# A decoder layer on one core: gated results transposed by DMA instead of TensorE, and low parts by accumulating DMAs in more blocks

## The chip, the core and the metric

The kernel runs on one core of a Trainium2 chip, in one launch. A core has engines with instruction streams of their own: TensorE (PE in the profile; PEld is its loading of the stationary operand), VectorE (DVE), ScalarE (ACT), GpSimd (POOL) and SyncE (SP). Each engine executes its instructions in order and waits on semaphores for the others. Transfers run on 16 DMA engines; they are issued from the streams of SP, ACT and POOL, also in order. The on-chip memory SBUF has 128 partitions; TensorE writes to PSUM, eight banks of 128x512 words of 32 bits.

The metric is the device time of a run in microseconds. The profile is one more execution, recorded instruction by instruction.

## What is computed

One layer of a decoder for 256 tokens of 2048 features, all in float32: a first gated feed-forward, two token mixers in parallel, a second gated feed-forward, and a gated embedding. The change touches the two feed-forwards:

```python
def swiglu(x, w_gu, w_down):
    g, u = jnp.split(x @ w_gu, 2, axis=-1)
    return (jax.nn.silu(g) * u) @ w_down
...
h = layer_norm(alpha * h + 0.5 * swiglu(h, w_ffn1_gu[i], w_ffn1_down[i]), ln_g[i, 0], ln_b[i, 0])
...
h = layer_norm(alpha * h + 0.5 * swiglu(h, w_ffn2_gu[i], w_ffn2_down[i]), ln_g[i, 2], ln_b[i, 2])
```

`x` is 256x2048, `w_gu` 2048x11264 (gate and up, 5632 columns each) and `w_down` 5632x2048. The middle of the layer (input projections, retention, attention, mixing) has the same form before and after the change.

## The kernel before, in words

**Numbers.** Every float32 operand is split into a high part in the matmul's own 32-bit format and a low part, the rest (`split`, L97 to L99: a copy on ScalarE at L98, a subtraction on VectorE at L99). A product is then three matmuls: low by high, high by high, high by low (`Sum.add`, L393 to L395).

**Weights.** They come in chunks of 128x1024 words, 512 KB, by DMAs from SP (L112). Four classes prepare them. `Single` (kind P) splits a chunk as above. `Folded` copies it to the high part on ScalarE (L162), writes the negated high part to the low tile on ScalarE (L163), and issues on POOL's queue a DMA that adds the raw chunk to it (L164): the subtraction runs in the DMA engines instead of VectorE. Kind F is a pair of one `Single` and one `Folded`, the gate's chunk and the up's chunk. `Seven` (kind S) takes the gate's and the up's chunk together and makes their four products of half blocks with seven products instead of eight: VectorE forms four sums (L189 to L192), and the parts are split on ScalarE and VectorE. `Prepared` (kind D) is the same with the sums made earlier in the run and loaded from HBM: six loads instead of two, and three splits.

**The gate and up stage.** A feed-forward handles its 5632 columns in eleven blocks, j = 0 to 10, of 512. A block has eight units, written as a string of eight letters by `gu_units` (L873 to L881): a unit P or F is two chunks of 12 matmuls each, a unit S or D one step of 21 matmuls. In the first feed-forward (names f1) blocks 1 to 10 are FFSSFSSF. In the second (f2) the blocks in `AHEAD` (1, 2, 3, 4, 5 and 7) are PPSDSDSP where j is odd and PPSSDSSP where j is even; block 6, 8 and 10 are PPSSPSSP and block 9 is PPSPSPSP. Block 0 has eight plain units in both.

**The end of a block.** The sums of the sevens are combined (`seven_common`), VectorE adds the rest from PSUM (L993), ScalarE applies Silu (L994) and VectorE multiplies gate and up (L995) into `v`: 256 tokens as two tiles of 128 partitions by 512 columns. The next stage needs it with the columns on the partitions. `turned` (L929 to L939) does that: eight transposes of 128x128 on TensorE into two PSUM banks (L937), and two copies on ScalarE into the tile `raw` of SBUF (L939). `convert` splits `raw` later, in the second stage (`w_down`), which starts with block 0's tile.

**The order.** No scheduler reorders: every stream has its instructions in the order in which the program's text issues them. After each chunk or step, `done` gives its SBUF slots back and calls `fill`, which issues the making of further chunks while the work made ahead is under 45 units (a chunk counts 12, a step 21), and loads while it is under 90. Then `run_side` takes one job from the list `side`. A job is put there by `later(n, job)`, as number n in the list (L1130 to L1134): the transposes of a block's result are issued with the third call of `run_side` in the next block, after its third chunk.

SBUF is shared out in 46 slots of 4 KB per partition (`SLOTS`); a new tile takes the slot that has been free longest, and its first writer waits for that slot's last reader.

Of the kernel before, what the change touches and what calls it, by code (L numbers as in the profile page):

```python
# [8 lines left out]
F32 = mybir.dt.float32  # L9
F32R = mybir.dt.float32r  # L10
I32 = mybir.dt.int32
AF = mybir.ActivationFunctionType
ALU = mybir.AluOpType
PSUM = bass.MemoryType.PSUM

P = 128
S = 256
# [23 lines left out]
SEVEN = (0, 1, 2, 3)  # L41

AHEAD = {1: (4, 5), 2: (4,), 3: (4, 5), 4: (4,), 5: (4, 5), 7: (4, 5)}
# [12 lines left out]
def layer(ctx: ExitStack, tc: tile.TileContext, io):  # L56
    nc = tc.nc
    sync, act, dve, pool, pe = nc.sync, nc.scalar, nc.vector, nc.gpsimd, nc.tensor
# [8 lines left out]
    def bank(name):  # L67
        return psum.tile([P, 512], F32, tag="ps", name=name)

    def banks(name):  # L70
        return [bank(name + str(j)) for j in range(2)]

    def slot(shape, dt, name):
        return slots.tile(shape, dt, tag="slot", name=name)

    def half(name):
        return slot([P, 2, 256], F32, name)
# [241 lines left out]
    def slots_for_weights(n, ahead=45, far=90):  # L319
        room.update(slots=n, ahead=ahead, far=far)  # L320
# [164 lines left out]
    def units_of(order, sevens, ahead=()):  # L485

        sevens, ahead = list(sevens), list(ahead)
        plain = [p for p in range(KD // 2) if p not in sevens + ahead]
        of = {"S": sevens, "D": ahead, "P": plain, "F": plain}
        return [(kind, of[kind].pop(0)) for kind in order]  # L490
# [61 lines left out]
    def rsqrt(dst, var, n, eps):  # L552
# [7 lines left out]
        )  # L560
        s = small.tile([P, n], I32, tag=f"ns{n}", name="ns", bufs=2)
        dve.tensor_scalar(s, v[:, 0].bitcast(I32), 1, None, ALU.logical_shift_right)
        y = small.tile([P, n], I32, tag=f"ny{n}", name="ny", bufs=2)
        dve.tensor_scalar(y, s, -1.0, float(0x5F3759DF - 2**31), ALU.mult, ALU.add)
# [37 lines left out]
    def ln_stats_by_root(stats, i, t, eps, between):  # L602
# [4 lines left out]
        root = small.tile([P, 1], F32, tag="nq1", name="nroot")  # L607
        act.activation(root, mv[:, 1:2], AF.Sqrt, bias=roots[eps], scale=4.0)
        v = small.tile([P, 1], F32, tag="nb1", name="nv")
# [10 lines left out]
    def table_of(f):  # L620

        act.activation(warm, warm, f)
# [29 lines left out]
    class Norm:  # L652
# [36 lines left out]
        def turn(self, t, c):  # L689

            args = self.y, t, self.i, self.new
            if c < 3 and (t, c + 1) != self.put_off:
                self.more(t, c + 1)
            self.sums_behind()
            if c == 0:
                for k0 in (0, 2):
                    ln_turn(*args, k0, 2, self.keep.get(c))
            else:
                ln_turn(*args, 4 * c, 4, self.keep.get(c))
# [19 lines left out]
        def run(self, steps, lhs, events, blks=(), calm=2):  # L719


            self.vectors = vectors.pop()
            table_of(AF.Sqrt)
            self.new = big.tile([P, KD, 512], F32R, tag="ht", name=f"ht{self.i}")
# [20 lines left out]
        def first(self, steps, lhs, sums, events):  # L745
# [14 lines left out]
            self.put_away()  # L760
            table_of(AF.Silu if self.i < 2 else AF.Sigmoid)

# [48 lines left out]
    ident = const.tile([P, P], F32, name="ident")  # L811
# [23 lines left out]
    def rotary_table(nm):  # L835

        inv, sgn = (0, 2) if nm == "r" else (1, 3)
        pos_i = slot([P, S], I32, "pos_i" + nm)
        act.dma_start(pos_i, io["positions"].broadcast_to([P, S]))
# [20 lines left out]
        yield  # L860
        act.activation(nb, n, AF.Sin)
        yield
# [5 lines left out]
        yield  # L868
        act.activation(cos, na, AF.Sin)
        yield  # L870


    def gu_units(name, j):  # L873
        if j == 0:
            return [("P", p) for p in range(KD // 2)]
        if name == "f2" and j in AHEAD:
            return units_of(*(("PPSDSDSP", SEVEN[:3]) if j % 2 else ("PPSSDSSP", SEVEN)), AHEAD[j])
        order = "PPSSPSSP" if j % 2 == 0 else "PPSPSPSP"
        if name == "f1":
            order = "FFSSFSSF"  # L880
        return units_of(order, SEVEN[: order.count("S")])  # L881

    def gu_keys(name, j):
        return lambda n, p: (name + "_gu", j, n, p)
# [34 lines left out]
    def ffn(name, i, ht, norm, keep, residual, keepers, away):  # L919
# [3 lines left out]
        raws = []  # L923
# [4 lines left out]

        def turned(j, v):  # L929

            raw = slot([P, 4, S], F32, f"{name}a{j}")
            raws.append(raw)
            ps = banks(f"{name}t{j}")
            for k in range(4):
                for t in range(2):
                    at = slice(k % 2 * S + t * P, k % 2 * S + t * P + P)
                    pe.transpose(ps[k // 2][:, at], v[:, t, k * P : (k + 1) * P], ident)  # L937
            for h in range(2):
                act.copy(raw[:, 2 * h : 2 * h + 2], ps[h].rearrange("p (b n) -> p b n", b=2))  # L939

        acts = {}

# [5 lines left out]
        for j in range(KF // 4):  # L948
            pg, pu = banks(f"{name}g{j}"), banks(f"{name}u{j}")
            units = gu_units(name, j)  # L950
            n_of = {(0, 0): KD, (0, 1): KD, (1, 0): KD, (1, 1): KD}
            for kind, p in units:
                if kind in "SD":
                    for at in ((0, 0), (0, 1), (1, 0)):
                        n_of[at] -= 1
                    n_of[1, 1] -= 2
            sums = [[Sum((pg, pu)[n][t], n_of[t, n]) for n in range(2)] for t in range(2)]
            got = []

            if norm is not None and j == 0:  # L960
                front, units = units[:FRONT_PAIRS], units[FRONT_PAIRS:]
                steps = [(gu_keys(name, 0)(n, p), 2 * p, n) for _, p in front for n in range(2)]
                norm.first(steps, rhs, sums, (
                    (3, (1, 0)), (5, "more"), (5, (1, 1)), (7, (0, 2)), (8, (1, 2)), (9, (0, 3)), (10, (1, 3)), (10, "go"),
                ))
                slots_for_weights(24)

            def before(u, j=j, offset=KD // 2 - len(units)):
                u += offset
                if j == 0 and norm is None and u % 2 == 0:  # L970
                    first_chunk(u // 2)
                    if u == 6:
                        slots_for_weights(24)
                    if u == 2:
                        load_constants()
                if j == 0 and u == 7:
                    for g in sorted({p // 2 for p in SEVEN}):
                        hi, lo = (slot([P, 8, P], F32R, f"{name}f{w}{g}") for w in "hl")
                        made[g] = seven_forms(keep[g], hi, lo)
                    if name == "f2":  # L980
                        g = AHEAD[1][0] // 2
                        made[g] = forms_of([ht[:, 4 * g : 4 * g + 4, :]], f"{name}f{g}")
                if name == "f2" and j in AHEAD and u == 0:
                    slots_for_weights(AHEAD_SLOTS - j)
                if j == KF // 4 - 1 and u in (4, 6):
                    convert(u // 2 - 2)

            block(f"{name}{j}", units, gu_keys(name, j), rhs, forms, sums, lambda *a: got.extend(seven_common(*a)), before)
            if got:
                g, v = got  # L990
                for x, ps in ((g, pg), (v, pu)):
                    for t in range(2):
                        dve.tensor_tensor(x[:, t], x[:, t], ps[t], ALU.add)  # L993
                act.activation(g, g, AF.Silu)  # L994
                dve.tensor_tensor(v, g, v, ALU.mult)  # L995
            else:
                v = slot([P, 2, 512], F32, f"{name}v{j}")
                for t in range(2):
                    act.activation(v[:, t], pg[t], AF.Silu)
                for t in range(2):  # L1000
                    dve.tensor_tensor(v[:, t], v[:, t], pu[t], ALU.mult)
            later(2, lambda j=j, v=v: turned(j, v))
        stats = small.tile([P, 2, 4, 6], F32, tag="stats", name=name + "st", bufs=1)

        def others(n, ahead=45):
# [77 lines left out]
    def joined(ps, name, dst=None):  # L1083
        lo = half(name + "lo")
        v = half(name + "v") if dst is None else dst
        for f in range(2):
            act.copy(lo[:, f], ps[f][:, S:])
            dve.tensor_tensor(v[:, f], ps[f][:, :S], lo[:, f], ALU.add)
        return v
# [40 lines left out]
    def later(n, job):  # L1130
        for j in range(n):
            if len(side) <= j:
                side.append(idle)
        side.insert(n, job)  # L1134
# [519 lines left out]
    def first_chunk(c):  # L1654

        if c == 0:
            load_x_chunk(0)
            fill()
        if c < 3:
            load_x_chunk(c + 1)  # L1660
# [157 lines left out]
```

## Time and profile before

| | |
|---|---|
| median of three runs | 2269.6 us (2269.53 to 2271.87) |
| the profiled execution | 2269.44 us |
| its span, first to last instruction | 2267.3 us |
| TensorE clock granted in it | 0.999 |
| moved by DMA | 536.69 MB, mean 237 GB/s |
| f1's gate and up stage, j = 1 to 10 | about 50 to 468 us of the span |
| f2's gate and up stage, j = 0 to 10 | about 1473 to 1933 us of the span |

How to read it. The span lies within the execution's own time; 2.1 us lie around it. A row of a group reads: line, engine, operation, output and inputs by the program's names, shapes, count | busy us, mean ns of one | idle time of that engine just before them, and what ended it. A row of a timeline reads: start in us, duration in us, engine, line, operation, names, count, and in brackets the idle time before it with its releaser. A row of a window reads: the stretch, its length, then busy us (and number of instructions) of PE, PEld, DVE, ACT and POOL, the granted clock, the share of time in which the 16 DMA engines were busy, and what they moved in GB/s. Matmuls are pipelined, so that durations of neighbours overlap; their distance is read from their starts.

### The profile page before, as it was taken

The numbers are of one execution on the slowest core, as the hardware profiler recorded it, in microseconds if no ns is written. First come the engines' busy times: TensorE is split into PE (matmuls) and PEld (weight loads), VectorE is DVE, ScalarE is ACT, GpSimd is POOL, SyncE is SP. The second block draws the span as 40 slices with busy tenths as digits, with TensorE's granted clock in tenths as the row PEclk, the third lists the DMA queues.
The fourth block names the chain that finished last, engine by engine and source line by source line (L and its number), as shares of the span: only waits on it lengthen the run. The fifth ranks groups of instructions, "written<-read, shape, count | busy, mean of one in ns | idle before, by whom it ended". The sixth has DMA issues, their size and how long they took to land.

```text
span 2267.3 us, 29270 instructions
## 1 busy us (share of the span) xinstructions
PE 2258.9 (100%) x10482; PEld 1877.7 (83%) x10482; DVE 1975.9 (87%) x2576; ACT 1272.5 (56%) x1543; POOL 37.1 (2%) x49
## 2 busy tenths in 40 slices
PE   9999999999999999999999999999999999999998
PEld 7888888888888888888778888888888888888887
DVE  7988989999989887888789788689999999889887
ACT  6676776656555444535566454455555565555543
POOL 0000010000000000000000000000000000000000
PEclk9999999999999999999999999999999999999999
DMA  9888898865677878775456568787867766555772
GB/s 316 249 261 252 238 262 243 250 208 186 216 285 261 291 282 289 256 236 183 140 158 225 183 211 293 271 288 247 297 242 250 255 197 218 196 190 209 290 269 73
DMA packets 216889, 536.69 MB, mean 237 GB/s; under 512 B 17052, under 2 KB 21532, under 8 KB 216744
## 3 DMA queue, kind: packets, MB, share of 16 engines
q1 hardware_dynamic: 209000, 511.28, 65.9%
q0 software_dynamic: 5760, 20.97, 5.1%
q10 hardware_dynamic: 1984, 2.58, 0.4%
q8 instruction: 82, 1.34, 0.2%
q14 instruction: 63, 0.52, 0.1%
HBM read 484.43 MB, written 29.36 MB: 227 GB/s over the span
## 4 chain that ended last, share of the span: by engine, by line
PE 78%; DVE 1%; DMA 1%; ACT 0%; issue 0%; ACTq 0%; DVEq 0%
PE f2g L395 3%; PE f2g L393 3%; PE f2g L394 3%; PE rqk L344 3%; PE f2u L393 2%; PE f2u L395 2%; PE f2u L394 2%; PE aqk L344 2%; PE f1d L395 2%; PE f2d L394 2%; PE f2d L395 2%; PE f1d L393 2%; PE f1d L394 2%; PE f2d L393 2%; PE f1e L395 1%; PE f2e L394 1%
## 5 line engine op out<-in xcount | busy, mean ns | idle before, releaser
L99 DVE TENSOR_TENSOR lf_gu<-rf_gu,hf_gu 128x1024 fp32r<-128x1024 f32 (+1 forms) x229 | 271.9, 1210 | 11.1 <-ACT hf_gu L98 10.4
L98 ACT CAST hf_gu<-rf_gu 128x1024 fp32r<-128x1024 f32 (+1 forms) x229 | 232.8, 1041 | 30.2 <-DMA rf_gu<-in_f_gu 29.9
L99 DVE TENSOR_TENSOR lf_down<-rf_down,hf_down 128x1024 fp32r<-128x1024 f32 x150 | 178.8, 1220 | 19.0 <-ACT hf_down L98 18.5
L99 DVE TENSOR_TENSOR lw_in_f<-rw_in_f,hw_in_f 128x1024 fp32r<-128x1024 f32 x140 | 167.5, 1220 | 25.0 <-ACT hw_in_f L98 24.7
L98 ACT CAST hf_down<-rf_down 128x1024 fp32r<-128x1024 f32 x150 | 151.7, 1049 | 50.7 <-DMA rf_down<-in_f_down 18.0
L98 ACT CAST huf_gu<-uf_gu 128x1024 fp32r<-128x1024 f32 x75 | 79.0, 1053 | 147.5 <-DVE uf_gu L190 138.0
L98 ACT CAST hw_in_f<-rw_in_f 128x1024 fp32r<-128x1024 f32 x140 | 140.3, 1050 | 3.2 <-PE rv L394 1.4
L98 ACT CAST hvf_gu<-vf_gu 128x1024 fp32r<-128x1024 f32 x75 | 79.1, 1055 | 31.7 <-DVE vf_gu L192 30.8
L99 DVE TENSOR_TENSOR luf_gu<-uf_gu,huf_gu 128x1024 fp32r<-128x1024 f32 x75 | 91.4, 1219 | 0.0
L99 DVE TENSOR_TENSOR lvf_gu<-vf_gu,hvf_gu 128x1024 fp32r<-128x1024 f32 x75 | 91.4, 1218 | 0.0
L393 PE MATMUL f1g<-hf_gu,xt 128*128 128x512 f32 x232 | 90.6, 390 | 0.2 <-ACT hf_gu L98 0.2
L395 PE MATMUL f1g<-lf_gu,xt 128*128 128x512 f32 x232 | 90.7, 391 | 0.0
L394 PE MATMUL f1g<-hf_gu,xt 128*128 128x512 f32 x232 | 90.4, 390 | 0.0
L393 PE MATMUL f2g<-hf_gu,ht 128*128 128x512 f32 x217 | 84.7, 390 | 0.0
L395 PE MATMUL f2g<-lf_gu,ht 128*128 128x512 f32 x217 | 84.7, 390 | 0.0
L394 PE MATMUL f2g<-hf_gu,ht 128*128 128x512 f32 x217 | 84.5, 390 | 0.0
L994 ACT ACTIVATE eve<-eve 128x1024 f32<-128x1024 f32 x20 | 21.2, 1061 | 100.4 <-DVE eve L993 100.4
L395 PE MATMUL f1u<-lf_gu,xt 128*128 128x512 f32 x192 | 75.0, 390 | 0.7 <-DMA lf_gu<-rf_gu 0.7
L393 PE MATMUL f1u<-hf_gu,xt 128*128 128x512 f32 x192 | 75.7, 394 | 0.0
L394 PE MATMUL f1u<-hf_gu,xt 128*128 128x512 f32 x192 | 74.9, 390 | 0.0
L393 PE MATMUL f2u<-hf_gu,ht 128*128 128x512 f32 x172 | 68.2, 397 | 0.0
L395 PE MATMUL f2u<-lf_gu,ht 128*128 128x512 f32 x172 | 67.1, 390 | 0.0
(1468 smaller groups left out, 6734.7 us busy)
## 6 DMA issues: line engine op xcount, KB each, us to landing
rf_gu<-in_f_gu SPq DMA_DIRECT2D x360, 512.0 KB
rf_down<-in_f_down SPq DMA_DIRECT2D x176, 512.0 KB
rw_in_f<-in_w_in_f SPq DMA_DIRECT2D x148, 512.0 KB
lf_gu<-rf_gu POOLq DMA_DIRECT2D x40, 512.0 KB, 7.0
rw_rv<-in_w_rv SPq DMA_DIRECT2D x32, 512.0 KB
rw_ret<-in_w_ret SPq DMA_DIRECT2D x32, 512.0 KB
rw_mix<-in_w_mix SPq DMA_DIRECT2D x32, 512.0 KB
rw_pg<-in_w_pg SPq DMA_DIRECT2D x32, 512.0 KB
```

The lines of the kernel that those rows point to most:

```text
L98: act.copy(dst_hi, src)
L99: (lo_engine or dve).tensor_tensor(dst_lo, src, dst_hi, ALU.subtract)
L344: pe.matmul(ps[f], hi[:, kk, f * P : (f + 1) * P], rhs(k), start=k == 0, stop=k == n_k - 1,)
L393: pe.matmul(o, al, bh, start=first, stop=False)
L394: pe.matmul(o, ah, bh, start=False, stop=False)
L395: pe.matmul(o, ah, bl, start=False, stop=self.left == 0)
L994: act.activation(g, g, AF.Silu)
```

## The change

Two things change.

First, `turned` has no matmuls. ScalarE copies the 16-bit halves of every 32-bit word of `v` apart, the low halves and the high halves into one tile `words` (two copies, 128x1024 words of 16 bits each). A transposing DMA on SP's queue, issued one call of `run_side` later, moves `words` to the tile `moved`, in squares of 128x128 16-bit words, sixteen in all. Three calls after that, two copies on ScalarE join the halves into `raw`. The job `turned` itself is put one place earlier in the list (1 instead of 2). That holds for the eleven blocks of both feed-forwards, 22 in all.

Second, `gu_units` gives other letters in f2. The blocks 4, 5 and 7 become FFSSDSSP, FFSDSDSP and FFSDSDSP; the blocks 6, 8, 9 and 10 become FFSSFSSP. So 18 more chunks are `Folded`, and block 9 has four units S where it had three. Blocks 0 to 3 of f2 and all of f1 keep their units.

```diff
+U16 = mybir.dt.uint16
...
         if name == "f2" and j in AHEAD:
-            return units_of(*(("PPSDSDSP", SEVEN[:3]) if j % 2 else ("PPSSDSSP", SEVEN)), AHEAD[j])
-        order = "PPSSPSSP" if j % 2 == 0 else "PPSPSPSP"
-        if name == "f1":
-            order = "FFSSFSSF"
+            plain = "P" if j < 4 else "F"
+            return units_of(*((f"{plain * 2}SDSDSP", SEVEN[:3]) if j % 2 else (f"{plain * 2}SSDSSP", SEVEN)), AHEAD[j])
+        order = "FFSSFSSP" if name == "f2" else "FFSSFSSF"
         return units_of(order, SEVEN[: order.count("S")])
...
         def turned(j, v):
-            raw = slot([P, 4, S], F32, f"{name}a{j}")
-            raws.append(raw)
-            ps = banks(f"{name}t{j}")
-            for k in range(4):
-                for t in range(2):
-                    at = slice(k % 2 * S + t * P, k % 2 * S + t * P + P)
-                    pe.transpose(ps[k // 2][:, at], v[:, t, k * P : (k + 1) * P], ident)
+            words = slot([P, 2, 2, 512], U16, f"{name}w{j}")
+            of_v = v.bitcast(U16).rearrange("p t (n h) -> p h t n", h=2)
             for h in range(2):
-                act.copy(raw[:, 2 * h : 2 * h + 2], ps[h].rearrange("p (b n) -> p b n", b=2))
+                act.copy(words[:, h], of_v[:, h])
+            moved = slot([P, 2, 2, 4, P], U16, f"{name}m{j}")
+
+            def turn():
+                sync.dma_start_transpose(
+                    moved.rearrange("p h t k n -> p (h t k) n"), words.rearrange("p h t n -> p (h t n)")
+                )
+
+            def joined():
+                raw = slot([P, 4, S], F32, f"{name}a{j}")
+                raws.append(raw)
+                of_raw = raw.bitcast(U16).rearrange("p k (t n h) -> p h t k n", t=2, h=2)
+                for h in range(2):
+                    act.copy(of_raw[:, h], moved[:, h])
+
+            later(0, turn)
+            later(3, joined)
...
-            later(2, lambda j=j, v=v: turned(j, v))
+            later(1, lambda j=j, v=v: turned(j, v))
```

## The prediction

> **What bounds the kernel now.** I read the page's busy table first, then the DMA queues, then windows that are one block of a feed-forward each, then timelines inside one block.
>
> ```profile
> span 2267.3 us, 29270 instructions
> ...
> PE 2258.9 (100%) x10482; PEld 1877.7 (83%) x10482; DVE 1975.9 (87%) x2576; ACT 1272.5 (56%) x1543; POOL 37.1 (2%) x49
> ...
> q1 hardware_dynamic: 209000, 511.28, 65.9%
> q0 software_dynamic: 5760, 20.97, 5.1%
> q10 hardware_dynamic: 1984, 2.58, 0.4%
> ```
>
> TensorE is never idle: 2258.9 of 2267.3 us. Whatever leaves its stream shortens the run, as long as nothing else becomes late. The windows (columns: PE, PEld, DVE, ACT, POOL busy, clock, DMA share, GB/s) show how close "else" is; the first two are blocks j=3 and j=7 of the first feed-forward (f1), then j=4, 6, 8, 9, 10 of the second (f2).
>
> ```profile
> 133.00:174.70 41.70, 41.70 (x190) 34.64 (x189) 37.60 (x46) 28.50 (x33) 3.44 (x4) 1.00 0.85 246
> 299.80:341.50 41.70, 41.70 (x190) 34.64 (x189) 37.62 (x46) 28.51 (x33) 3.44 (x4) 1.00 0.90 247
> ...
> 1642.30:1683.30 41.00, 41.00 (x186) 34.08 (x185) 40.41 (x49) 22.70 (x27) 0.00 (x0) 1.00 0.78 274
> ...
> 1724.30:1766.00 41.70, 41.70 (x189) 34.64 (x188) 41.11 (x49) 23.54 (x28) 0.00 (x0) 1.00 0.74 240
> 1807.10:1848.80 41.70, 41.70 (x190) 34.63 (x189) 41.11 (x49) 24.39 (x28) 0.00 (x0) 1.00 0.66 214
> 1848.80:1891.10 42.30, 42.30 (x192) 35.15 (x191) 38.47 (x46) 24.25 (x28) 0.00 (x0) 1.00 0.59 187
> 1891.10:1932.80 41.70, 41.70 (x189) 34.65 (x188) 41.05 (x48) 24.96 (x29) 0.00 (x0) 1.00 0.66 218
> ```
>
> In f1 the second limit is DMA: 0.85 x 41.7 = 35.4 us of work per block, up to 0.90 x 41.7 = 37.5. In f2's even blocks it is VectorE, 41.1 of 41.7 us.
>
> **The transposes that leave TensorE.** The line's own view counts them, and the timeline of block j=3 prices them.
>
> ```profile
> L937 PE MATMUL f1t<-ident,evw x80: 271/273/273, 99.7 to 476.9; 128*128 128x128 f32 x80
> L937 PE MATMUL f2t<-ident,evw x80: 271/273/273, 1568.7 to 1942.0; 128*128 128x128 f32 x80
> L937 PE MATMUL f1t<-ident,f1v x8: 271/272/273, 58.0 to 58.7; 128*128 128x128 f32 x8
> L937 PE MATMUL f2t<-ident,f2v x8: 270/273/273, 1527.6 to 1528.4; 128*128 128x128 f32 x8
> ```
>
> ```profile
> 140.48 0.39 PE L395 MATMUL f1g<-lf_gu,xt 128*128 128x512 f32 x1
> ...
> 141.16 0.40 PE L395 MATMUL f1g<-lf_gu,xt 128*128 128x512 f32 x1
> 141.39 1.03 PE L937 MATMUL f1t<-ident,evw 128*128 128x128 f32 x8
> ...
> 142.50 0.40 PE L394 MATMUL f1u<-hf_gu,xt 128*128 128x512 f32 x1
> ```
>
> Three matmuls take 141.16 - 140.48 = 0.68 us, 0.227 each. From 141.16 to 142.50 is 1.34 us where two steps would be 0.45: eight transposes cost 0.89 us. There are 176 = 22 x 8, so 22 x 0.89 = **19.6 us** leave the stream.
>
> **A fourth product of seven in f2's j=9.** Its order changes from three S and five plain pairs to four S and four. A plain pair is 24 matmuls, an S 21: 3 x 0.227 = **0.7 us** less on TensorE. VectorE pays for an S five operations of 0.685 and three of 1.21, 7.1 us, against 2.4 for the pair; three folded chunks give back 3.6. So 38.5 us becomes 39.6 of about 40.8: hidden.
>
> ```profile
> L189 DVE TENSOR_TENSOR uf_gu<-rf_gu,rf_gu 128x512 f32<-128x512 f32 x75 | 51.4, 685 | 6.3 <-DMA rf_gu<-in_f_gu 6.3
> L99 DVE TENSOR_TENSOR lf_gu<-rf_gu,hf_gu 128x1024 fp32r<-128x1024 f32 (+1 forms) x229 | 271.9, 1210 | 11.1 <-ACT hf_gu L98 10.4
> ```
>
> **What ScalarE gets.** Per block two evictions (0.586 each) go; two 16-bit copies before the DMA and two after it come, all 128x1024.
>
> ```profile
> L939 ACT COPY f1a<-f1t 128x512 f32<-128x512 f32 x22 | 11.7, 585 | 4.6 <-PE f1t L937 4.6
> L98 ACT CAST huf_gu<-uf_gu 128x1024 fp32r<-128x1024 f32 x75 | 79.0, 1053 | 147.5 <-DVE uf_gu L190 138.0
> L163 ACT ACTIVATE lf_gu<-hf_gu 128x1024 fp32r<-128x1024 f32 x40 | 42.5, 1062 | 1.3
> ```
>
> No row has a 16-bit copy with a stride. Below, 0.585 (the same bytes); above, twice the 1.05 of a 1024-element cast; I take 1.05, the nearest by elements. That adds 4 x 1.05 - 1.17 = 3.0 us per block. The cover is ScalarE's waiting for VectorE's sums:
>
> ```profile
> 138.13 1.06 ACT L98 CAST hvf_gu<-vf_gu 128x1024 fp32r<-128x1024 f32 x1 [0.40 <-DVE vf_gu L192]
> 139.09 1.04 ACT L98 CAST hf_gu<-rf_gu 128x1024 fp32r<-128x1024 f32 x1
> ...
> 143.40 1.05 ACT L98 CAST huf_gu<-uf_gu 128x1024 fp32r<-128x1024 f32 x1 [2.75 <-DVE uf_gu L190]
> ...
> 153.67 1.05 ACT L98 CAST hf_gu<-rf_gu 128x1024 fp32r<-128x1024 f32 x1
> ...
> 157.87 1.05 ACT L98 CAST huf_gu<-uf_gu 128x1024 fp32r<-128x1024 f32 x1 [2.64 <-DVE uf_gu L190]
> ```
>
> By the order in which `fill` and `run_side` issue, the first two copies stand after the cast at 138.13 (done near 141.3), ahead of the one at 139.09 and a half-size one behind it; both still end before 143.40. The joining copies stand ahead of 153.67 and end near 155.8; 157.87 is still met. So ScalarE costs nothing. At 2.1 us a copy each insertion overruns its 2.7 us gap by about 1.5 us, 3 us per block; VectorE waits for those casts, with TensorE behind it.
>
> **The DMA itself** moves 512 KB from SBUF to SBUF, 22 times, on SP's queue. Its price is not in the trace. Below: a plain 512 KB load, 0.659 x 2267.3 us x 0.524 / 511.28 = 1.53 us of all 16 engines. Next: an accumulating one, 0.051 x 2267.3 / 40 = 2.9 us. Above: moved as 256-byte rows (128 words), 2048 pieces at q10's mean packet, 0.004 x 16 x 2267.3 / 1984 = 73 ns: 9.4 us. I take 2.5, nearest to the accumulating row, which also reads and writes SBUF. The Trainium skill's DMA: Bandwidth & Descriptors, section Latency and other measured facts, gives a transposing DMA 261 GB/s; by that it would be an estimated 2.0 us, and the sum would come out about a microsecond lower. No trace here shows it.
>
> SP executes in order. The DMA stands behind the loads starting at 130.70 and ahead of those at 135.91, and waits for the copies until about 141.3:
>
> ```profile
> 130.70 2.02 SPq L112 DMA_DIRECT2D rf_gu<-in_f_gu  x2
> 135.91 0.89 SPq L112 DMA_DIRECT2D rf_gu<-in_f_gu  x2
> 138.86 0.37 SPq L112 DMA_DIRECT2D rf_gu<-in_f_gu  x1
> 142.13 0.37 SPq L112 DMA_DIRECT2D rf_gu<-in_f_gu  x1
> ```
>
> The slipped ones' first use, and the DMA share in between:
>
> ```profile
> 156.55 0.68 DVE L189 TENSOR_TENSOR uf_gu<-rf_gu,rf_gu 128x512 f32<-128x512 f32 x1
> ...
> 142.10:149.90 7.80, 7.80 (x38) 6.50 (x36) 7.73 (x11) 6.12 (x8) 0.00 (x0) 1.00 0.25 74
> ```
>
> Four loads slip to about 144 us (SP's hold for the new DMA bounded by 0.37 us, a plain issue, and 9.4, the whole transfer; I take 2). The first is used at 156.55, and the DMA engines are 0.25 busy from 142.1 to 149.9: 5.9 us free for the transfer and the slipped loads. The transfer lands before 150, the joining copies want it near 153.8: hidden, with 4 us to spare. Were it later, the casts of the fourth S would stand behind the joining copies on ScalarE, VectorE behind those, then TensorE. POOL's queue is not passed. Of SBUF's 46 slots the program text counts at most 43 in use here (25 for weights, ten results, six of sums, two of the block); two more fit.
>
> **The folded chunks of f2**: two each in j=4, 5, 7, three in j=6, 8, 9, 10, eighteen in all. Each takes 1.21 us off VectorE (21.8 in sum), adds 1.06 on ScalarE and 2.9 of DMA. TensorE gains nothing from that; it matters since a TensorE 0.89 us faster leaves an even block 40.8 us, where VectorE has 41.1 of work. What is late next is the landing, as f1 shows, where such chunks exist:
>
> ```profile
> 150.16 0.86 POOL L164 DMA_DIRECT2D lf_gu<-rf_gu  x1 [20.87 <-DVE lf_gu L99]
> 157.70 0.39 PE L395 MATMUL f1u<-lf_gu,xt 128*128 128x512 f32 x1
> DMA to landing us min/median/max: 4.9/7.0/10.3
> ```
>
> Issue to use is 7.54 us, landing 7.0. In the new order the issue comes 1.07 earlier (evictions gone) and the use 0.89 earlier: 7.7 against 7.0 to 10.3. I charge 0.3 us per f1 block, 3 us. In f2's j=5 and 7, with two D pairs of six loads each, I take it that loads land just in time (L189, which starts an S, waited 6.3 us for DMA, the only such wait in its row); 2.5 us more ahead of them I charge with 1.5 us per block, 3 us.
>
> **Sum**, against the profiled execution's 2269.44 us (the median is 2269.6): 2269.4 - 19.6 - 0.7 + 6.0 = **2255**. All hidden: 2249.
>
> **Rivals.**
> *Late landings.* DMA work per block becomes 37.5 + 2.5 = 40.0 of 40.8 us in f1, and landings move toward 10.3. At 8.7 us the chunk above is 1.0 us late in ten f1 and four f2 blocks: 2249 + 14 + 3 = 2266. For it: the DMA share of 0.90. Against: 5.9 of block j=3's 6.3 us of DMA idle lie just where the transfer goes.
> *A slow transposing DMA*, the one that ends slower: its time of all engines decides, from 41.7 - 37.5 = 4.2 us on. At 6 us an f1 block takes up to 43.5, ten of them +18; f2's j=4 (32.0 + 5.8 + 6) +2.8, j=6 (30.9 + 8.7 + 6) +3.9, the rest about -1.5: 2293. At 9.4 us it is +3.4 in each of some 18 blocks more, near 2350. For it: no row shows 16-bit scatter. Against: bytes and direction are those of the 2.9 us row. The Trainium skill's VectorE: DVE Perf Modes, section The three transpose paths, speaks for it: 1309 ns for a 128x128 square by DMA against 390 ns on TensorE; sixteen squares one after another would be an estimated 21 us, far beyond all that I take. TensorE's own row here, eight in 0.89 us with 32-bit data, is far under its 390, so I trust the other too only as a latency.
> *VectorE sets the pace*, so that the change gives nothing in f2: 2249 + 10 + 6 = 2265. For: 41.11 of 41.70. Against: the folded chunks take 2.4 to 3.6 us per block off it, from j=4 on.
>
> **Chances.** Forecast 0.60 (its own range 2247 to 2264); late landings 0.13; slow DMA 0.23, a quarter of it near 2350; VectorE 0.04. A measurement tells 0.2%, 4.5 us, from no change. Faster 0.60; same 0.15 (late landings and VectorE lie at its edge); slower 0.25. The range runs from 2247 to 2293, where the slow DMA stands at 6 us; beyond it I leave some 0.13, below 0.03.
>
> **What would show it.** L937 gone and f1 blocks of 40.8 us, f2's of 40.1 and 40.8; the new SP issues landing within about 5 us; ScalarE's wait for `moved` near nothing; L164 58 times, and TensorE's wait for `lf_gu` DMAs a few us in total. Wrong if the DMA share of an f1 block reaches 1.0 with blocks over 41.7, or if ScalarE's joining copies wait for their DMA.

## The result and the profile after

The changed kernel takes 2258.75 us (median of five runs, 2257.79 to 2260.33) against 2269.6 us before: ratio 0.9949, 95% interval 0.9936 to 0.9962. That is 10.9 us less; the forecast was 2255, 14.4 below the profiled execution of before, with its own range from 2247 to 2264. The profiled execution has a span of 2255.8 us, 11.5 less than before.

The page of the changed kernel, its busy table, DMA queues and accumulating issues:

```profile
span 2255.8 us, 29093 instructions
...
PE 2241.5 (99%) x10303; PEld 1857.3 (82%) x10303; DVE 1960.8 (87%) x2564; ACT 1366.8 (61%) x1607; POOL 52.6 (2%) x67
...
q1 hardware_dynamic: 254760, 522.82, 68.7%
q0 software_dynamic: 8352, 30.41, 7.0%
...
lf_gu<-rf_gu POOLq DMA_DIRECT2D x58, 512.0 KB, 7.8
```

TensorE's time outside its busy time rose from 8.4 us to 14.3. The view of waits says for what it stood (engine, line, what was awaited: us in total, times, longest):

```profile
PE f2u L396 <- DMA lf_gu<-rf_gu: 4.5, 5, 1.7
PE f1u L396 <- DMA lf_gu<-rf_gu: 2.4, 4, 1.1
```

Before there was one such wait of 0.7 us. All nine are for folded chunks, `lf_gu`, whose low part an accumulating DMA makes. The view counts only the idle part of a wait; the timeline shows its whole price:

```profile
400.76 0.39 PE L395 MATMUL f1u<-hf_gu,xt 128*128 128x512 f32 x1
402.22 0.50 PE L396 MATMUL f1u<-lf_gu,xt 128*128 128x512 f32 x1 [1.07 <-DMA lf_gu<-rf_gu]
402.55 0.39 PE L394 MATMUL f1u<-hf_gu,xt 128*128 128x512 f32 x1
```

Two starts that would be 0.23 apart are 1.46 apart, and the next follows after 0.33: 1.3 us for 1.07 of idle time. So the nine waits cost some 6.9 + 9 x 0.26 = 9.2 us, the one of before some 1.0, and 8.2 is new. With the 20.3 us that the prediction took off TensorE, 12.1 us should be gained; 11.5 are.

Windows, one block each, from a block's first matmul of S to the next block's: j=3 and j=7 of f1, then j=4 to 9 of f2 (columns: PE, PEld, DVE, ACT, POOL busy, clock, DMA share, GB/s):

```profile
142.48:183.28 40.80, 40.80 (x181) 33.78 (x180) 37.50 (x46) 31.98 (x35) 3.44 (x4) 1.00 0.95 270
306.69:347.49 40.80, 40.80 (x181) 33.78 (x180) 37.59 (x46) 32.01 (x35) 3.44 (x4) 1.00 0.96 268
...
1643.44:1684.27 40.83, 40.44 (x178) 33.15 (x177) 38.90 (x47) 30.05 (x34) 1.72 (x2) 1.00 0.89 274
1684.27:1725.98 41.71, 40.46 (x178) 33.15 (x177) 34.28 (x42) 26.81 (x30) 1.74 (x2) 1.00 0.97 309
1725.98:1767.55 41.57, 41.12 (x182) 33.71 (x181) 38.88 (x47) 32.00 (x35) 2.59 (x3) 1.00 0.92 273
1767.55:1809.84 42.29, 40.60 (x179) 33.06 (x177) 34.49 (x43) 27.24 (x29) 1.72 (x2) 1.00 0.96 301
1809.84:1850.64 40.80, 40.80 (x182) 33.78 (x180) 38.39 (x47) 30.73 (x34) 2.61 (x3) 1.00 0.88 255
1850.64:1891.44 40.80, 40.80 (x182) 33.78 (x180) 38.59 (x47) 30.89 (x34) 2.58 (x3) 1.00 0.91 257
```

Where nothing is late, f1's blocks are 40.8 us (41.7 before) and f2's 8 and 9 too. VectorE fell to 38.9 us and less. The DMA share of these two blocks of f1 rose from 0.85 and 0.90 to 0.95 and 0.96. The loss stands in the stretches that begin with blocks 4 to 7 of f2, with shares up to 0.97: without a wait, the stretches of 4, 5 and 7 would be 41.0 - 0.9 = 40.1 us and that of 6 would be 40.8.

Last, the new pieces themselves: the two sorts of copies on ScalarE, and the transposing DMA, for which the duration is the time that SP's queue is held (least, median, most):

```profile
L948 ACT COPY f1a<-f1m 128x1024 uint16<-128x1024 uint16 x22 | 28.3, 1355 | 0.0
...
L935 ACT COPY f1w<-evw 128x1024 uint16<-128x1024 uint16 x20 | 19.9, 1040 | 0.0
```

```profile
L939 SPq DMA_TRANSPOSE f1m<-f1w x11: 1322/1874/3547, 57.5 to 468.0; - x11
```

The joining copies never waited for `moved` (0.0 idle in their row). L937 is gone, and the accumulating issues number 58, as said.

### The profile page after: what moved, and what is told of

Same layout as the page of the kernel before. It is cut to its first block, busy times and chain, and to the rows that moved or that the text cites. A ratio compares the mean times of both kernels' runs of the same rounds, so it can differ in the third digit from the quotient of the medians.

```text
span 2255.8 us, 29093 instructions
## 1 busy us (share of the span) xinstructions
PE 2241.5 (99%) x10303; PEld 1857.3 (82%) x10303; DVE 1960.8 (87%) x2564; ACT 1366.8 (61%) x1607; POOL 52.6 (2%) x67
## 3 DMA queue, kind: packets, MB, share of 16 engines
q1 hardware_dynamic: 254760, 522.82, 68.7%
## 4 chain that ended last, share of the span: by engine, by line
PE 90%; DMA 5%; issue 2%; DVE 2%; ACT 1%; ACTq 0%; POOLq 0%; SPq 0%; DVEq 0%
DMA lf_gu<-rf_gu 3%; PE rqk L345 3%; PE f1g L394 2%; PE f1g L396 2%; PE f1g L395 2%; PE f1u L396 2%; PE f1u L395 2%; PE f1u L394 2%; PE f2g L396 2%; PE f2g L395 2%; PE f2g L394 2%; DMA rf_gu<-in_f_gu 2%; PE f2u L396 2%; PE f2u L395 2%; PE f2u L394 2%
## 5 line engine op out<-in xcount | busy, mean ns | idle before, releaser
L100 DVE TENSOR_TENSOR lf_gu<-rf_gu,hf_gu 128x1024 fp32r<-128x1024 f32 (+1 forms) x210 | 250.2, 1208 | 15.5 <-ACT hf_gu L99 14.7
L99 ACT CAST hf_gu<-rf_gu 128x1024 fp32r<-128x1024 f32 (+1 forms) x210 | 214.4, 1038 | 33.6 <-DMA rf_gu<-in_f_gu 32.2
L165 POOL DMA_DIRECT2D lf_gu<-rf_gu x58 | 50.2, 866 | 1845.9 <-DMA rf_gu<-in_f_gu 1253.0
```

Source lines behind the costliest of these rows:

```text
L99: act.copy(dst_hi, src)
L100: (lo_engine or dve).tensor_tensor(dst_lo, src, dst_hi, ALU.subtract)
L165: pool.dma_start(c.lo, c.raw, accum_op=ALU.add)
```

## The experiments

Each timed run has its ratio to the kernel before, with its interval. The first four take the parts apart.

**The transposing DMAs alone.** The diff puts the units of before back:

```diff
-            return units_of(*((f"{plain * 2}SDSDSP", SEVEN[:3]) if j % 2 else (f"{plain * 2}SSDSSP", SEVEN)), AHEAD[j])
-        order = "FFSSFSSP" if name == "f2" else "FFSSFSSF"
+            return units_of(*(("PPSDSDSP", SEVEN[:3]) if j % 2 else ("PPSSDSSP", SEVEN)), AHEAD[j])
+        order = "PPSSPSSP" if j % 2 == 0 else "PPSPSPSP"
+        if name == "f1":
+            order = "FFSSFSSF"
```

> The transposing DMAs alone; the second feed-forward keeps the units of the kernel before (no folded chunks, three S in block 9). Theory (what was given back are TensorE's waits for the accumulating DMAs of folded chunks, 5.8 us of them in the second feed-forward): the 5.8 us are gone, the plain pair of block 9 costs 0.7, VectorE's 41.1 us of work in blocks of 40.8 costs 1 to 2 us: 2255 us, below the changed kernel's 2258.8. Rival 'VectorE sets the pace': the even blocks 4, 6, 8, 10 stay at 41.1 us or more and the plain ones wait with them: 2259 or more. Rival 'the transposing DMAs themselves delay what TensorE waits for': waits for other tiles take the place of those for folded chunks, 2258 to 2260.

2261.8 us, ratio 0.9963 (0.9950 to 0.9975). The theory's 2255 lies outside that interval (2255 / 2270.05 = 0.9934); the rival "VectorE sets the pace" holds. TensorE's waits in f2 are now for VectorE; the longest of them:

```profile
PE f27s L396 <- DVE lf_gu L100: 1.1, 1, 1.1
PE f26s L396 <- DVE luf_gu L100: 0.8, 1, 0.8
```

```profile
1811.99:1854.84 42.85, 41.67 (x181) 33.56 (x180) 42.26 (x50) 28.37 (x32) 0.00 (x0) 1.00 0.64 196
```

In that window of block 8 VectorE is busy for 42.26 of 42.85 us, and DMA has fallen to 0.64. The folded chunks' waits cost f2 5.8 us (below), the plain pair of block 9 0.7; without the chunks and with the pair the run is 3 us longer, so that VectorE costs some 5.8 + 3.0 - 0.7 = 8 us by the medians. (The intervals of this run and of the changed kernel overlap; that it isn't 4 us faster is clear of them, that it is slower is not.)

**The new units alone.** The kernel before, with the changed kernel's units in f2:

```diff
-            return units_of(*(("PPSDSDSP", SEVEN[:3]) if j % 2 else ("PPSSDSSP", SEVEN)), AHEAD[j])
+            plain = "P" if j < 4 else "F"
+            return units_of(*((f"{plain * 2}SDSDSP", SEVEN[:3]) if j % 2 else (f"{plain * 2}SSDSSP", SEVEN)), AHEAD[j])
...
+        order = "FFSSFSSP" if name == "f2" else "FFSSFSSF"
```

> The second feed-forward's new units alone; the transposes stay on TensorE. Theory (the folded chunks are late because the DMA engines are full with transposes and accumulations together): without the transposes the waits of 5.8 us in the second feed-forward shrink to some 2, the fourth S gives 0.7: 2271 us, 1 slower than the kernel before. Rival 'the chain load, copy, accumulation is too long by itself': all 5.8 us stay, 2274 to 2275. Rival 'VectorE was the limit': 2268 or less.

2269.65 us, ratio 0.9997 (0.9988 to 1.0006): no change, between the theory's 2271 and 2268. The f2 part of the change does nothing alone, and no wait for a folded chunk of f2 appears: without transposing DMAs the accumulations are in time.

**No transfer.** The copies stay, the DMA goes (the transposition is left out):

```diff
-            moved = slot([P, 2, 2, 4, P], U16, f"{name}m{j}")
+            moved = words.rearrange("p h t (k n) -> p h t k n", k=4)
...
-            later(0, turn)
```

> Leaves the transposition out: ScalarE's four 16-bit copies stay, the second two read what the first two wrote, and no DMA runs between them. Theory (the transfer's time on the DMA engines delays the accumulations): the first feed-forward's waits fall from 3.5 us to 1 or less, the second's from 5.8 to 2 or 3: 2252 to 2254 us. Rival 'ScalarE's copies or the shorter blocks bring the delay': 2257 to 2259, with the same waits at the same chunks.

2250.85 us, ratio 0.9919 (0.9905 to 0.9932). One wait for a folded chunk is left:

```profile
PE f1u L396 <- DMA lf_gu<-rf_gu: 1.4, 1, 1.4
```

So the 7.9 us between this run and the changed kernel (6.8 by the ratios, whose intervals don't meet) come from the transfers, and not from ScalarE's four copies, which are all there, nor from the shorter blocks. The run also has one tile fewer in SBUF's slots (`moved`), and no run takes that apart from the transfer; the plain copy below keeps the tile. 2250.85 is also close to the prediction's 2249 for "all hidden".

**The transfer twice**, into two tiles, one of them unused:

```diff
+                again = slot([P, 2, 2, 4, P], U16, f"{name}n{j}")
+                sync.dma_start_transpose(
+                    again.rearrange("p h t k n -> p (h t k) n"), words.rearrange("p h t n -> p (h t n)")
+                )
```

> Each transposing DMA runs twice, into two tiles, of which one is used. Theory (a transfer takes 2.75 to 2.95 us of all DMA engines and the first feed-forward's blocks have only some 2 us left): its blocks go from 40.8 to between 41.7 and 43.4 us, blocks 4 to 8 of the second each up to 2 us longer: 2265 to 2290 us, 2275 in the middle. Rival 'a transfer lies in idle time whatever it takes': 2259 to 2262.

2303.6 us, ratio 1.0149 (1.0135 to 1.0162), above the range of 2265 to 2290. Each of the 22 added transfers costs 44.8 / 22 = 2.0 us of the run. That isn't the transfer's engine time alone: the second one also holds SP once more, and the mean clock granted to TensorE is 0.993 in this profile instead of 0.999, which is an estimated 0.006 x 2301 = 14 of the 44.8 us (the last section says what the clock does behind a wait).

The next two ask what about the transfer makes the accumulations late: its time on the DMA engines, or SP, which stands until the words are there. The two after them take work off the DMA engines.

**A sixteenth of the transfer**, at the same place (the transposition is left out):

```diff
-            moved = slot([P, 2, 2, 4, P], U16, f"{name}m{j}")
+            moved = words.rearrange("p h t (k n) -> p h t k n", k=4)
+            part = slot([P, 2, 2, 4, P], U16, f"{name}m{j}")
...
-                    moved.rearrange("p h t k n -> p (h t k) n"), words.rearrange("p h t n -> p (h t n)")
+                    part.rearrange("p h t k n -> p (h t k) n")[:, :1], words.rearrange("p h t n -> p (h t n)")[:, :P]
```

> Leaves the transposition out, as in the run without a transfer, but a sixteenth of the transposing DMA runs at its place: SP waits for the same copies and its loads slip by the same time, while the transfer takes 0.2 us of all DMA engines instead of 2.95. Theory (it is the transfer's engine time that makes the accumulations late): 2251 us as without a transfer, at most one wait over 0.5 us for a folded chunk in each feed-forward. Rival 'it is SP's wait, behind which the loads pile up': 2257 to 2259, with the waits of the changed kernel.

2260.9 us (five runs from 2256.0 to 2261.4), ratio 0.9953 (0.9941 to 0.9966), above the run without a transfer. Its queue carries (212520 - 209000) / 22 = 160 packets more per block instead of (254760 - 209000) / 22 = 2080, and the loss is still there: the transfer's engine time alone isn't the cause. The wait isn't quite the one that was expected, though: this transfer reads words of the first of the two copies only, and is issued when that one is done, 0.9 us before the second:

```profile
136.97 1.99 ACT L935 COPY f1w<-evw 128x1024 uint16<-128x1024 uint16 x2
```

```profile
138.04 1.09 SPq L940 DMA_TRANSPOSE f1m<-f1w  x1
```

What SP's wait does is seen in the changed kernel's block 3. SP's timeline first (the rows of loads are groups, from the first's start to the last's end):

```profile
124.09 8.94 SPq L113 DMA_DIRECT2D rf_gu<-in_f_gu  x3
139.48 1.79 SPq L939 DMA_TRANSPOSE f1m<-f1w  x1
141.37 9.76 SPq L113 DMA_DIRECT2D rf_gu<-in_f_gu  x6
```

SP stands from 133.03 to 139.48, then holds for 1.79. Windows of 4 us there, of the changed kernel and then of the run without a transfer:

```profile
133.00:137.00 4.00, 4.00 (x19) 3.34 (x18) 3.93 (x6) 1.55 (x2) 0.00 (x0) 1.00 0.93 303
137.00:141.00 4.00, 4.00 (x19) 3.30 (x19) 4.00 (x5) 3.92 (x5) 0.00 (x0) 1.00 0.10 25
141.00:145.00 4.00, 4.00 (x20) 3.30 (x19) 3.93 (x7) 2.83 (x3) 0.00 (x0) 1.00 1.07 214
145.00:149.00 4.00, 4.00 (x19) 3.34 (x18) 4.00 (x5) 3.69 (x5) 0.86 (x1) 1.00 0.99 263
```

```profile
133.00:137.00 4.00, 4.00 (x19) 3.30 (x19) 3.93 (x6) 1.67 (x2) 0.00 (x0) 1.00 1.03 332
137.00:141.00 4.00, 4.00 (x20) 3.30 (x19) 4.00 (x6) 3.79 (x5) 0.00 (x0) 1.00 1.02 341
141.00:145.00 4.00, 4.00 (x19) 3.34 (x18) 3.93 (x6) 2.95 (x3) 0.00 (x0) 1.00 0.11 40
145.00:149.00 4.00, 4.00 (x20) 3.30 (x19) 4.00 (x5) 3.57 (x5) 0.86 (x1) 1.00 0.47 136
```

With the transfer SP stands, the engines run dry (share 0.10 from 137 to 141), and the loads behind it fill the stretch after it. Without it the loads are done by 141, and the idle stretch lies where the third folded chunk's accumulation is issued (a POOL busy time of 0.86 in the fourth row of each). In the changed kernel it meets full engines, and lands 7.0 us after its issue instead of 5.7. In block 3 that is still in time. All four waits of f1 are for this third folded chunk, in blocks 4, 6, 9 and 10; in block 9, with the longest, it lands after 8.7 us instead of 4.8.

**A plain copy** of the same bytes at the same place (the transposition is left out):

```diff
-                sync.dma_start_transpose(
-                    moved.rearrange("p h t k n -> p (h t k) n"), words.rearrange("p h t n -> p (h t n)")
-                )
+                sync.dma_start(moved, words.rearrange("p h t (k n) -> p h t k n", k=4))
```

> Leaves the transposition out: a plain DMA of the same 512 KB from SBUF to SBUF runs at the place of the transposing one. If the bytes and the direction make the price, it takes 2.7 us or more of all DMA engines and the time is the changed kernel's, 2257 to 2259. If the 256-byte pieces make it, it takes 1.5 to 1.7 us and the waits shrink to about half: 2253 to 2255.

2254.6 us, ratio 0.9932 (0.9919 to 0.9946). By the share of its queue, 67.2% of 2254.0 us against 66.2% of 2248.0 without a transfer, it takes 26.5 / 22 = 1.2 us; the transposing one, 68.7% of 2255.8, takes 61.5 / 22 = 2.8. It waits for the words as the changed kernel does, and its interval overlaps both that of the changed kernel and that of the run without a transfer, so it doesn't settle how the 7.9 us divide. Beside the sixteenth it is a puzzle: it has the longer wait and more than twice the engine time (the sixteenth's share, 66.4% of 2258.8 us, gives 0.5 us), and is 6.3 us faster by the medians.

**Fewer folded chunks in f1, others in f2:**

```diff
-        order = "FFSSFSSP" if name == "f2" else "FFSSFSSF"
+        order = ("PFSSFSSF" if j in (6, 8) else "FFSSFSSP") if name == "f2" else "FFSSPSSF"
```

> First feed-forward with three folded chunks a block instead of four (the one behind the second S is plain); blocks 6 and 8 of the second keep three but the first folded one becomes the last. Theory: with 2.7 us of DMA less per block and the tightest chunk plain, the first feed-forward's waits fall from 3.5 us to 1, VectorE has 38.7 us of work in 40.8 and stays hidden; in the second the waits of 1.5 and 2.0 us at the first folded chunk of blocks 6 and 8 go: 2253 us. Rival 'VectorE sets the pace' (1.21 more on it per block): first feed-forward's blocks at 41 to 41.5 us, 2257 to 2261. Rival 'the lateness moves to the next block's transfers': block 7's S waits, 2256 to 2258.

2267.9 us, ratio 0.9988 (0.9979 to 0.9997). Less DMA made it slower than the changed kernel. TensorE's waits for folded chunks are 5.2 us in f1 and 5.8 in f2: in f1 for the last one of the late blocks, in f2 the longest, 3.2, for the one that was moved to the end of block 6. So neither the theory nor "VectorE sets the pace" was right, and taking a chunk from the DMA doesn't by itself bring the next one in time.

**Two results of f2 turned on TensorE**, with f1's units as in the run above:

```diff
+            if name == "f2" and j in (4, 6):
...
+                        pe.transpose(ps[k // 2][:, at], v[:, t, k * P : (k + 1) * P], ident)
...
-            later(1, lambda j=j, v=v: turned(j, v))
+            later(2 if name == "f2" and j in (4, 6) else 1, lambda j=j, v=v: turned(j, v))
```

> First feed-forward with three folded chunks a block as in the run beside it; in the second the results of blocks 4 and 6 are transposed on TensorE again, 0.89 us each, so that blocks 5 and 7, whose DMA share was 0.96 to 0.97, have no transposing DMA. Theory: the first feed-forward gives 2.5 us; the waits of 1.5 and 2.0 us behind blocks 5 and 7 go and 1.8 us of transposes come: 2254.5 us. Rival 'those waits come from the blocks' own loads': they stay, 2258.

2263.1 us, ratio 0.9968 (0.9956 to 0.9979). f1 lost as above (5.7 us of waits). In f2 the waits fell from 4.5 to 1.8 us, as expected, but 1.8 us of transposes came for it: about a microsecond is won there.

The last four move the transfer, to let SP reach it when the words are there.

```diff
-            later(0, turn)
-            later(3, joined)
+            later(1, turn)
+            later(4, joined)
```

> The transposing DMA is issued one unit of TensorE's work later (two loads further back in SP's order), the joining copies one unit later too. Theory now (SP waits 3 to 8 us at the transposing DMA for the 16-bit words, the DMA engines run dry for some 4 us, and the loads behind it then run together with the accumulations): from the loads' times in the run without a transfer SP would reach the DMA 0 to 4 us before the words instead of 3 to 8; about half of the loss goes: 2255 us. Rival 'the transfer's engine time': nothing changes, 2258 to 2259. Rival 'nearer to the accumulation at the sixth unit': 2260 or more.

2273.4 us, ratio 1.0017 (1.0008 to 1.0026).

> The transposing DMA two units later (four loads), the joining copies one unit later. Theory: in most blocks SP reaches the DMA after the words are there, no stretch of idle DMA engines ahead of it is left, what remains is the transfer's own 2.95 us: 2252 to 2253 us. Rival 'the transfer's engine time': 2258 to 2259. Rival 'nearer to the accumulation at the sixth unit', which it now directly precedes: folded chunk 6 late in most blocks of the first feed-forward, 2260 or more.

This one has `later(2, turn)`. 2272.4 us, ratio 1.0010 (1.0001 to 1.0019). In both, the theory and the first rival fell: they are 14 us slower than the changed kernel. The times lie where the rival "nearer to the accumulation" had them, which had no upper bound. They don't show its mechanism, since two causes were tangled: the joining copies had moved too. The next run keeps these where they were:

```diff
-            later(0, turn)
+            later(1, turn)
```

> The transposing DMA one unit later, the joining copies where the changed kernel has them. Two causes are left for the 14 us that the run with both a unit later lost. Theory (the joining copies, moved, stood on ScalarE right ahead of the fourth folded chunk of a block of the first feed-forward, whose accumulation was issued 1.6 to 2.4 us nearer to its use): that lead is back at 7.7 us, the third folded chunk lands in 5.5 to 6 us, 2252 to 2256 us. Rival 'SP's hold at the transposing DMA' (3.4 us in the mean instead of 2.3 where the DMA engines are busy when it is issued, loads held behind it): the loss stays, 2265 to 2273.

2262.9 us (2260.6 to 2267.8), ratio 0.9968 (0.9955 to 0.9980): most of the loss came from the joining copies, which had stood ahead of the fourth folded chunk's copies on ScalarE; but no gain is left. Two windows of its profile (the slowest of its runs), f1's blocks 3 to 5 and then 6 to most of 10, and SP's holds in f1 with the DMA one unit later:

```profile
142.30:264.70 122.40, 122.40 (x541) 101.42 (x540) 112.66 (x136) 95.59 (x103) 10.33 (x12) 1.00 0.98 268
264.70:460.00 195.30, 189.21 (x822) 154.92 (x821) 175.85 (x209) 151.22 (x161) 15.58 (x18) 0.99 0.95 255
```

```profile
L939 SPq DMA_TRANSPOSE f1m<-f1w x11: 1785/3959/6537, 56.5 to 471.4; - x11
```

For three blocks TensorE waits for nothing, at a DMA share of 0.98. Then 6 us go. Over f1's eleven transfers the hold is 3.96 us in the median, up to 6.5, instead of 1.87 and 3.5, and the loads stand behind it. So SP's wait in the changed kernel seems to have a good side: the engines run empty in it, and the transfer passes more quickly.

**From ScalarE's queue**, at the end of the next block, with the joining copies a block later:

```diff
-                sync.dma_start_transpose(
+                act.dma_start_transpose(
...
-            later(0, turn)
-            later(3, joined)
+            later(8 if name == "f2" and j in (0, 1, 2, 3, 4, 6) else 9, turn)
+            later(14, joined)
```

> The transposing DMAs leave SP's queue: ScalarE issues each at the end of the next block, behind the fourth folded chunk's copies and ahead of the Silu there, where it waited 2.3 us for VectorE in the changed kernel; the joining copies keep their place in a block, one block later. SP neither waits for the words nor is held by the transfer. Theory (SP's standing, 8 us per block, runs the DMA engines dry and bunches the loads behind it; the transfer's own engine time matters only in blocks that are full): the third folded chunk lands in 5.5 to 6 us as without a transfer, at most two waits over 0.5 us in each feed-forward, 2251 to 2254 us. Rival 'the transfer's engine time': the waits stay, 2257 to 2259. Rival 'ScalarE is held instead': the hold, 2.3 us or more while the engines are busy, delays the casts of the next block's first S and VectorE behind them, 2260 or more.

2403.1 us, ratio 1.0570 (1.0548 to 1.0592), far beyond the 2260 from which the rival "ScalarE is held instead" counted. ScalarE is held: one of the longest holds on its timeline, and all of f1's:

```profile
174.65 13.56 ACTq L939 DMA_TRANSPOSE f1m<-f1w  x1
188.26 1.06 ACT L1006 ACTIVATE eve<-eve 128x1024 f32<-128x1024 f32 x1 [12.55 <-issue]
```

```profile
L939 ACTq DMA_TRANSPOSE f1m<-f1w x11: 1555/6688/14082, 84.0 to 596.2; - x11
```

But the hold isn't what TensorE waits for. Its waits, 76.3 us in f1 and 45.1 in f2, are for folded chunks, and the long ones for a chunk whose copies were done and whose accumulation was issued just behind a transposing DMA. This one belongs to the hold above (POOL, TensorE and ScalarE):

```profile
176.06 0.86 POOL L165 DMA_DIRECT2D lf_gu<-rf_gu  x1 [4.16 <-ACT lf_gu L164]
```

```profile
204.11 0.80 PE L396 MATMUL f1u<-lf_gu,xt 128*128 128x512 f32 x1 [13.88 <-DMA lf_gu<-rf_gu]
```

```profile
204.10 1.04 ACT L163 CAST hf_gu<-rf_gu 128x1024 fp32r<-128x1024 f32 x1 [2.12 <-DMA f1m<-f1w]
```

The accumulation lands 28.0 us after its issue, at the time at which the transposing DMA lands too (ScalarE's wait for `f1m` ends there). So much of the time went to accumulations that ran beside the transfer, which neither the theory nor a rival had named. The mean clock granted fell to 0.973.

The same transfer holds its queue for 6.7 us in the median and up to 14 when it runs beside SP's loads. The Trainium skill's DMA: Bandwidth & Descriptors, section Queues, rings and completion order, says that each DMA engine takes turns between queues packet by packet; pieces of 256 bytes against loads' pieces of 2 KB and more would then get a small share, if a packet has about as many pieces in both. The rows agree with that, but don't show it: no run here varied the size of the pieces on that queue.

Of the versions that still transpose, none beats the changed kernel.

## Why the prediction was right, and where it was off

**TensorE's gain: right.** The eight transposes were taken at 0.89 us per block; f1 blocks without a wait went from 41.70 to 40.80. The fourth S of block 9 came as worked out, and the run without a transfer ends within 2 us of "all hidden".

**The transfer's price: right in size.** 2.5 us of all engines were taken; its queue's share gives 2.8. The slow transposing DMA, with 0.23 the largest rival, did not come: 2.8 is under the 4.2 from which it was to decide. The Trainium skill's 1309 ns for one square (VectorE: DVE Perf Modes, section The three transpose paths) would have been an estimated 21 us for sixteen in turn; SP was held for 1.87, and the joining copies never waited.

**ScalarE: right in f1.** Splitting copies took 1.04 us as assumed, joining ones 1.36 instead of 1.05, so 3.6 us per block instead of 3.0, and the run without a transfer shows that they are hidden when nothing else is late. In f2 they aren't quite free: behind a late load they stand ahead of a folded chunk's copies (the rows below), and no run separates what that costs.

**SP's wait: the step that failed.** The prediction had SP wait for the words, four loads slip, and took 5.9 us of DMA idle time from 142 to 150 as free for both. The wait came, until 139.48. But it emptied the engines ahead of the transfer (0.10), and what had been idle behind it became full (0.99 and more). The idle time moved to where nothing used it. The same stretch was the cover of the accumulation issued in it, that of the third folded chunk, for which TensorE waits in blocks 4, 6, 9 and 10. The prediction looked for a place for the transfer, not at who else used that place.

**The late landings: right in mechanism, mis-sized in f2.** The sum charged 3 us in f1 and 3 us in f2 (1.5 each in blocks 5 and 7). By idle time and 0.26 per wait, f1 lost 2.4 + 4 x 0.26 - 1.0 = 2.4; f2 lost 4.5 + 5 x 0.26 = 5.8. In f1 the prediction had priced the right chunk.

In f2 it had the right two places, and there the loads do come later: in blocks 5 and 7 ScalarE waits 6.49 and 6.81 us for one, against 4.33 and 5.71 before. What TensorE then waits for is the first folded chunk of the next block, whose copies stand behind on ScalarE. Here is block 7's load, with the joining copies and that chunk's last copy, and then the chunk's accumulation and the matmul that waited:

```profile
1780.22 1.05 ACT L99 CAST hf_gu<-rf_gu 128x1024 fp32r<-128x1024 f32 x1 [6.81 <-DMA rf_gu<-in_f_gu]
...
1785.38 2.58 ACT L948 COPY f2a<-f2m 128x1024 uint16<-128x1024 uint16 x2
...
1791.75 1.06 ACT L164 ACTIVATE lf_gu<-hf_gu 128x1024 fp32r<-128x1024 f32 x1
```

```profile
1793.30 8.64 DMA lf_gu<-rf_gu
...
1801.98 0.50 PE f2u L396
```

These two waits, 1.25 and 1.69 us idle, cost 3.5 with their 0.26 each, close to the 3 charged. The other 2.3 us are three shorter waits for folded chunks of blocks 5, 6 and 10, for which the sum had no term in f2.

Landing rose from a median of 7.0 us to 7.8, not to the rival's 8.7.

**VectorE sets the pace: rightly set aside, for the reason given.** With the folded chunks VectorE's even blocks are at 38.9 us and less. Without them it does set the pace, and costs some 8 us, near the 10 of the prediction's rival.

**What stays open** is how the 7.9 us divide between SP's standing and the transfer's engine time. The sixteenth shows that as much can be lost with 0.5 us of engine time; but the plain copy, in which SP stands as long as in the changed kernel, loses only about half, so that standing alone doesn't explain the sixteenth either. The double transfer adds engine time, hold and clock together, and moving the transfer exchanged SP's wait for its hold. The single waits differ from run to run: the five times of the sixteenth spread over 5.4 us, those of the first two moved versions over 6 to 10.

## What to carry to other kernels

Work taken off the engine that sets the pace and given to DMA was paid here in latency of the transfers that were just in time, not in bytes: look for those with the least lead. A DMA that waits for a result, put in a queue that carries loads, stops the loads behind it, and the DMA time lost while it waited was not had back in the idle stretch behind it, because another transfer lived on that stretch. Two parts of a change may each do little and only pay together: here the DMA transposes gave 8 us alone, the relief of VectorE nothing alone, and both 11 (by the medians; the intervals of 8 and 11 overlap).

## What the hardware showed that was not expected

A wait of TensorE can cost more than itself and the 0.26 us. After one of 2.6 us idle in the run with the DMA one unit later, the granted clock fell (windows during and after), and matmuls started 0.43 us apart instead of 0.23:

```profile
448.10:452.50 4.40, 4.40 (x12) 3.51 (x13) 4.34 (x6) 3.93 (x4) 0.00 (x0) 0.61 0.94 385
452.50:456.00 3.50, 3.50 (x17) 2.85 (x16) 3.50 (x4) 3.47 (x5) 0.86 (x1) 1.00 0.05 7
```

```profile
448.10 0.50 PE L396 MATMUL f1u<-lf_gu,xt 128*128 128x512 f32 x1 [2.60 <-DMA lf_gu<-rf_gu]
...
449.60 0.63 PE L395 MATMUL f1u<-hf_gu,xt 128*128 128x512 f32 x1
450.03 0.63 PE L396 MATMUL f1u<-lf_gu,xt 128*128 128x512 f32 x1
```

Some 1.7 us more are lost (12 matmuls in 4.40 us where 0.227 each would be 2.7). In the changed kernel, whose longest wait is 1.7 us, it did not happen. The length of the wait alone doesn't decide it. In the run with a sixteenth of the transfer the clock stayed at 1.00 after a wait of 2.7 us, and fell after one of 2.5. In the run with fewer folded chunks it fell after one of 1.95 us, and stayed after the longest, 3.2 (windows behind the two):

```profile
463.20:466.60 3.40, 3.40 (x10) 2.62 (x9) 2.48 (x4) 1.58 (x2) 0.00 (x0) 0.50 0.47 190
1761.70:1766.00 4.30, 4.30 (x19) 3.56 (x20) 2.30 (x3) 0.49 (x1) 0.00 (x0) 1.00 1.05 257
```

No run here shows what decides it. The lower clock is part of what the slow versions lose. The Trainium skill's TensorE: Matmul & The Clock Gate, section Part 1: The HAM clock gate, has half the clock after an idle window of about 3.4 us; here waits of 2.6 and of 1.95 us had it behind them.
